# Order of splits, squares and first sums in the rounds of a norm ahead of a wide feed-forward stage

## The chip, the cores and the metric

The kernel runs on one core of a Trainium2 chip, in float32 throughout. A core has a matrix engine (TensorE, PE in the profile, with its weight loads as PEld), a vector engine (VectorE, DVE), a scalar engine (ScalarE, ACT), a general engine (GpSimd, POOL) and a queue that issues transfers (SyncE, SP). Each works through its own list of instructions in order and waits for the others through semaphores. The metric is the time of one execution on the device in microseconds (us), as the median of several runs.

## The reference

Two transformer blocks in a row, over 1024 tokens of width 1024. Each has a mixer (attention of two kinds in the first; a pooling mixer and a neighbourhood attention in the second), an output projection added to the residual x, a norm, and a feed-forward part. The part at issue is the last one, which both blocks have:

```python
# first block, D_FF = 2816
x = x + jnp.einsum('bse,ed->bsd', mixed, w_out[l])
h = rms_norm(x, ffn_norm_g[l])
g = jnp.einsum('bsd,df->bsf', h, w_gate[l])
u = jnp.einsum('bsd,df->bsf', h, w_up[l])
x = x + jnp.einsum('bsf,fd->bsd', jax.nn.silu(g) * u, w_down[l])
...
# second block, D_FF_2 = 4096
x = x + jnp.concatenate([a, b], axis=-1) @ w_out[l]
h = rmsnorm(x, norm_mlp_g[l])
x = x + jnp.square(jax.nn.relu(h @ w_up[l])) @ w_down[l]
```

`rms_norm` multiplies each row by one over the root of its mean square (with 1e-6 added), and each column by a gain.

## The kernel before

The residual x lies in eight tiles of 128 tokens by 1024 columns. Matrix products run on operands in a faster float format. To keep float32 precision, each operand is split into a high part h, a copy of the source in that format, and a low part l, the source less h; a product is then three, h by h, h by l and l by h. `split` (L113) does this: the copy on ACT (L114), the subtraction on DVE or, if asked, on POOL (L115).

The wide stage, the product of the normed x with the gate and up weights (or the up weights alone), is `ffn` (L873), called once in each block. It doesn't multiply the matrices directly. It cuts both into quadrants and forms seven products instead of eight, of sums and differences of quadrants. The tokens' side gives seven operands, named `b11` and `b21` (plain quadrants of the first four tiles: left and right half of the columns), `b22` (a plain quadrant of the last four), and `t1` to `t4` (differences). The weights' side gives `a11`, `a12`, `a22` and `s1` to `s4`. A unit is 256 columns of weights; there are 22 in the first block and 16 in the second.

Ahead of the units stand eight rounds, one for each tile t (L934 to L952). A round does the following.

- `down` (L179): PE multiplies the last quarter of the mixer's output with the last quarter of the output weights, 12 matmuls into two PSUM banks, and DVE adds these to x[t] (L195).
- x[t] is stored to `xd`, by SP (L936), since the scaling below overwrites it.
- ACT squares x[t] and sums each row (L938); POOL makes the mean (L939) and takes the power -1/2 (L941).
- DVE scales the tile of the round before, x[t-1], by its factor and the gain (`scaled`, L931).
- In rounds 3 to 6, the tile x[t-3], long scaled, is made into its share of `b11` and `b21` by two calls of `turn_split` (L778): PE transposes four blocks into a PSUM bank (L782), ACT copies the high part, DVE subtracts for the low part.
- In some rounds a weight piece is loaded (`load_raw`, L786).
- Half of a unit's `a11`, `a12` is split (`w_split`, L791): the copy on ACT, the subtraction on POOL.

Behind the rounds come `sums(0)`, `scaled(7)`, the first products `p1(0)` and `p1(1)`, and so on (L974 to L993). `sums(j)` (L961) forms, in place where it can, the differences of tile j and tile j+4: two subtractions on DVE, then two on POOL that read what the first two wrote (L732). `turn(j)` (L970) makes the five operands `b22`, `t1`, `t2`, `t3`, `t4` of these by five calls of `turn_split`; the last two read what POOL wrote. `p1(i)` (L915) is the product of `a11` and `b11` for unit i, whose result ACT copies aside (L920); `p2(i)` (L922) adds that of `a12` and `b21`. `w_sums` (L797) forms the differences of a unit's weights on POOL, and `w_rest` (L807) splits them; the main loop over the units follows at L1021.

What sets the order: the whole of this part runs under a manual schedule (L912 to L1131 for ACT, DVE, POOL and SP, L1513 for PE), so each engine's list has the instructions in the order in which the program names them. The PSUM has eight banks, taken through `one` (L107).

Of the kernel before, what the change touches and what calls it, by code (L numbers as in the profile page):

```python
# [11 lines left out]
AF = mybir.ActivationFunctionType  # L12
ALU = mybir.AluOpType
# [4 lines left out]
NT = 8  # L18
NK = 8
S = 1024  # L20
EPS = 1e-6
# [64 lines left out]
class Kern:  # L86
# [786 lines left out]
    def ffn(self, x, xd, mxd, wo, close_w, gi, n, gated, wts, wd, md, finish):  # L873


        nc, tc = self.nc, self.tc
        E = mybir.EngineType
        L = self.AHEAD
# [7 lines left out]
        slot = lambda: op.tile([P, 4, 512], F32R, tag="o", name="o")  # L886
        two = lambda tag: (aB.tile([P, 4, 512], F32R, tag=tag + "h", name=tag + "h"),
                           aB.tile([P, 4, 512], F32R, tag=tag + "l", name=tag + "l"))
# [5 lines left out]
        ops = [(pair(a_[0]), pair(a_[1]), [(pair(w_[0])[:, k, :], pair(w_[1])[:, k, :]) for k in range(2)])]  # L894
        jg = f32(flat(slot()))
        self.acts = {"b11": (slot(), slot()), "b21": (slot(), slot())}
        junk, g = jg[:, :S], jg[:, S:]
# [12 lines left out]
        us = [{"use": f} for f in users]  # L910
        first = lambda i: self.load_raw(wts[i][:, :1024])
# [16 lines left out]
        raws = [first(0), first(1)]  # L928
        r = [None] * NT

        def scaled(t):  # L931
            nc.vector.scalar_tensor_tensor(x[t], x[t], r[t], g, ALU.mult, ALU.mult)

        for t in range(NT):  # L934
            self.down(x, ops, t)
            nc.sync.dma_start(xd[t], x[t])  # L936
            ss, v = self.stat(), self.stat()
            nc.scalar.activation(junk, x[t], AF.Square, accum_out=ss)  # L938
            nc.gpsimd.tensor_scalar(v, ss, 1.0 / S, EPS, ALU.mult, ALU.add)  # L939
            r[t] = self.stat()  # L940
            nc.gpsimd.tensor_tensor(r[t], v, self.mhalf, ALU.pow)  # L941
            if t:
                scaled(t - 1)
            if 3 <= t < 7:
                self.turn_split(x[t - 3][:, :512], "b11", t - 3)
                self.turn_split(x[t - 3][:, 512:], "b21", t - 3)
            if t in (2, 4, 6):
                raws.append(first(t // 2 + 1) if t < 6 else self.load_raw(wts[0]))
            k = t % 2
            self.w_split(us[t // 2], ("a11", "a12")[k], raws[0][:, k * 512:(k + 1) * 512], True)  # L950
            if k:
                raws.pop(0)  # L952
        raws.append(first(L))

        for nm in ("t2", "t3"):
            self.acts[nm] = (slot(), slot())
        for nm in ("b22", "t1", "t4"):
            self.acts[nm] = two(nm)
        ts = [None] * 4

        def sums(j):  # L961
            lo, hi = x[j], x[j + 4]
            t2 = misc.tile([P, 512], F32, tag="y", name="t2s", bufs=6)
            self.sub(lo[:, :512], hi[:, :512], lo[:, :512], False)
            self.sub(t2, hi[:, 512:], lo[:, :512], False)
            self.sub(hi[:, :512], hi[:, 512:], hi[:, :512])
            self.sub(lo[:, 512:], t2, lo[:, 512:])
            ts[j] = (("b22", hi[:, 512:]), ("t1", lo[:, :512]), ("t2", t2), ("t3", hi[:, :512]), ("t4", lo[:, 512:]))
# [2 lines left out]
            for nm, src in ts[j]:  # L971
                self.turn_split(src, nm, j)

        sums(0)  # L974
        scaled(7)
        p1(0)
        p1(1)
# [812 lines left out]
```

## Time and profile before

| | |
|---|---|
| median of 3 runs | 2293.58 us (2292.99 to 2294.38) |
| the profiled execution | 2293.09 us |
| its span in the profile | 2291.3 us |
| mean granted clock of TensorE | 0.992 of full |
| mean DMA rate | 150 GB/s |
| rounds of the norm, first block | about 585 to 616 us from the span's start |
| rounds of the norm, second block | about 1612 to 1643 us from the span's start |

The span is the time from the first to the last instruction in the profile, and the execution's time is a little longer. A row of a timeline has the start in us, the duration in us, the engine, the line, the operation, what it writes and reads, and how many instructions were merged into the row (x2); in brackets stands how long the engine was idle before it, and what ended that. A row of busy time by stretch has the stretch, its length, each engine's busy time with the number of instructions, the granted clock of PE as a share of full, the share of DMA and its rate in GB/s. Successive instructions of an engine overlap a little in the records (about 0.1 us), since each is shown up to the end of its last write; so the step from one start to the next is somewhat shorter than the duration.

### The profile page before, as it was taken

What the parts mean: (1) busy time and instruction counts of PE and PEld (TensorE: products, weight loads), DVE (VectorE), ACT (ScalarE), POOL (GpSimd) and SP (SyncE); (2) the same over time, 40 slices, a digit from 0 to 9 for tenths busy, and PEclk for the clock granted to TensorE, in tenths of its full rate; (3) what the DMA queues carried; (4) which work ended last, traced back from release to release, by engine and by line L of the source; (5) the groups of instructions that cost most, each with busy time, mean ns of one, the idle gap of its engine ahead of it and who ended that gap; (6) DMA issues with size and microseconds to landing.
All of it is one profiled execution on the core that took longest, in us unless ns stands there. A gap on an engine that the chain in (4) does not pass through costs nothing.

```text
span 2291.3 us, 30717 instructions
## 1 busy us (share of the span) xinstructions
PE 2209.7 (96%) x11148; PEld 1869.7 (82%) x11148; DVE 1494.5 (65%) x2510; ACT 996.4 (43%) x1826; POOL 810.6 (35%) x742
## 2 busy tenths in 40 slices
PE   8999999989999999999999899999999998999998
PEld 8888898867788888878887888888778887878886
DVE  6356666677754545457889725687744445688888
ACT  5245555644442323223333536663454444434333
POOL 1055656564432322242235302120432223233335
PEclk9999999999999999999999999999999999999999
DMA  6386574651424433346321379883335543633202
GB/s 243 131 223 202 157 214 143 193 172 51 166 72 142 135 115 108 116 143 244 133 69 55 86 208 264 230 256 130 120 118 166 166 139 138 275 147 129 74 37 83
DMA packets 129193, 343.43 MB, mean 150 GB/s; under 512 B 12681, under 2 KB 49929, under 8 KB 114193
## 3 DMA queue, kind: packets, MB, share of 16 engines
q1 hardware_dynamic: 128896, 341.20, 45.7%
q8 instruction: 88, 1.44, 0.3%
q14 instruction: 65, 0.52, 0.1%
q10 hardware_dynamic: 144, 0.26, 0.0%
HBM read 254.35 MB, written 87.06 MB: 149 GB/s over the span
## 4 chain that ended last, share of the span: by engine, by line
PE 70%; DVE 15%; issue 5%; POOL 4%; ACT 4%; DMA 2%; SPq 0%; ACTq 0%; DVEq 0%; POOLq 0%
PE one L743 27%; PE one L1233 16%; PE one L163 11%; PE one L175 5%; DVE o L115 4%; PE one L189 4%; DVE x L195 1%; PE one L288 1%; PE one L582 1%; DVE x L1238 1%; DVE e L243 1%; PE one L230 1%; PE one L231 1%; DVE wl L115 1%; PE one L1414 1%
## 5 line engine op out<-in xcount | busy, mean ns | idle before, releaser
L1233 PE MATMUL one<-o 128*128 128x512 f32 x2268 | 519.3, 390 | 12.3 <-DVE o L115 12.2
L1233 PEld LDWEIGHTS one<-o 128*128 128x128 f32 x2268 | 424.3, 188 | 106.2 <-DVE o L115 18.4
L743 PE MATMUL one<-o,wh 128*128 128x512 f32 x1216 | 308.0, 396 | 17.1 <-DVE u L1042 8.7
L115 DVE TENSOR_TENSOR wl<-raw,wh 128x512 fp32r<-128x512 f32 (+2 forms) x254 | 206.0, 825 | 137.3 <-ACT wh L114 137.2
L743 PEld LDWEIGHTS one<-o,wh 128*128 128x128 f32 x1216 | 230.3, 191 | 69.2 <-ACT f L861 7.0
L114 ACT ACTIVATE wh<-raw 128x512 fp32r<-128x512 f32 (+2 forms) x278 | 185.7, 698 | 78.6 <-POOL raw L732 46.2
L732 POOL TENSOR_TENSOR s<-raw 128x512 f32<-128x512 f32 x38 | 54.9, 1446 | 443.2 <-DMA raw<-in_wgu_dram 208.1
L743 PE MATMUL one<-o,wl 128*128 128x512 f32 x608 | 164.4, 393 | 0.0
L247 ACT ACTIVATE e<-e,st 128x768 f32<-128x768 f32 (+7 forms) x128 | 99.4, 776 | 134.8 <-DVE st L243 131.7
L1238 DVE TENSOR_TENSOR x<-x,one 128x512 f32<-128x512 f32 x184 | 121.8, 677 | 50.6 <-PE one L1233 50.4
L743 PEld LDWEIGHTS one<-o,wl 128*128 128x128 f32 x608 | 115.6, 190 | 24.4
L163 PE MATMUL one<-actH,wh 128*128 128x512 f32 x448 | 122.8, 396 | 0.2 <-DVE ptl L115 0.2
L163 PE MATMUL one<-actL,wh 128*128 128x512 f32 x448 | 122.8, 396 | 0.0
L163 PE MATMUL one<-actH,wl 128*128 128x512 f32 x448 | 122.4, 395 | 0.0
L1394 POOL TENSOR_SCALAR ne<-ne,st 128x384 f32<-128x384 f32 x64 | 39.3, 614 | 220.7 <-DVE st L249 209.8
L1062 DVE TENSOR_TENSOR u<-one,p 128x512 f32<-128x512 f32 x38 | 26.3, 691 | 138.6 <-PE one L743 138.6
L114 ACT ACTIVATE o<-tb 128x1024 fp32r<-128x1024 f32 (+1 forms) x42 | 42.7, 1030 | 164.9 <-DVE tb L732 164.9
L735 POOL TENSOR_TENSOR sa<-mq 128x1024 f32<-128x1024 f32 (+1 forms) x14 | 35.4, 2545 | 196.4 <-DVE o L115 52.9
L565 POOL TENSOR_SCALAR b<-negc,cT 128x640 f32<-128x640 f32 (+3 forms) x64 | 49.8, 779 | 153.3 <-DVE st L243 94.8
L732 POOL TENSOR_TENSOR raw<-raw 128x512 f32<-128x512 f32 x76 | 99.3, 1306 | 6.0
L845 ACT ACTIVATE f<-f 128x512 f32<-128x512 f32 x33 | 20.9, 632 | 184.3 <-DVE f L838 167.1
L861 ACT ACTIVATE f<-f 128x512 f32<-128x512 f32 x48 | 30.3, 632 | 156.1 <-DVE f L838 126.8
(256 smaller groups left out, 5006.5 us busy)
## 6 DMA issues: line engine op xcount, KB each, us to landing
raw<-in_wgu_dram SPq DMA_DIRECT2D x22, 1024.0 KB, 5.3
raw<-in_wup_dram SPq DMA_DIRECT2D x16, 1024.0 KB, 5.4
mr<-f SPq DMA_DIRECT2D x64, 256.0 KB, 4.5
raw<-in_wdn_dram SPq DMA_DIRECT2D x12, 1024.0 KB, 4.9
wq<-in_wdn_dram SPq DMA_DIRECT2D x12, 1024.0 KB, 8.8
nbias<-in_nab_dram SPq DMA_DIRECT2D x32, 384.0 KB, 4.3
mq<-mr SPq DMA_DIRECT2D x12, 1024.0 KB, 9.8
raw<-in_wgu_dram SPq DMA_DIRECT2D x22, 512.0 KB, 3.8
```

The costliest lines, as they stand in the source:

```text
L114: self.nc.scalar.activation(h, src, AF.Copy)
L115: (self.nc.gpsimd if pool else self.nc.vector).tensor_tensor(l, src, f32(h), ALU.subtract)
L163: self.nc.tensor.matmul(ps, lhsT=w_[:, k, cols:cols + P], rhs=ac[:, 4 * j + k, half * 512:half * 512 + 512], start=(n == 0), stop=(n == 23))
L175: self.nc.tensor.matmul(ps, lhsT=ac[:, 4 * j + k, t * P:(t + 1) * P], rhs=w_[:, k, :], start=(n == 0), stop=(n == 23))
L189: nc.tensor.matmul(dst[h], lhsT=a_[:, kk, t * P:(t + 1) * P], rhs=w_[:, h * 512:(h + 1) * 512], start=(n < 2), stop=(n >= last))
L247: nc.scalar.activation(e, e, AF.Exp, bias=mx, scale=-1.0, accum_out=sm)
L565: nc.gpsimd.tensor_scalar(b[:, :nk], nc_row[:, :nk], cT[:, qt, h:h + 1], 1.0, ALU.add, ALU.mult)
L732: (self.nc.gpsimd if pool else self.nc.vector).tensor_tensor(out, a, b, ALU.subtract)
L743: self.nc.tensor.matmul(ps, lhsT=l, rhs=r, start=(first and n == 0), stop=(n == total - 1), skip_group_check=True)
L1233: nc.tensor.matmul(ps, lhsT=l[:, sl], rhs=r[:, sb], start=(start and n == 0), stop=(n == total - 1), skip_group_check=True)
L1238: nc.vector.tensor_tensor(dst, dst, ps, op)
L1394: nc.gpsimd.tensor_scalar(e[:, hf, :], e[:, hf, :], r, 1.0, ALU.mult, ALU.mult)
```

## The change

In rounds 3 to 6 the two calls of `turn_split` move from behind the scaling to ahead of the square. `sums(0)` moves from behind the loop into round 7, ahead of the square, the mean, the power, and the scaling of x[6]; for this, the functions `sums` and `turn` are defined ahead of the loop. Nothing else changes: the same instructions are issued, on the same engines.

```diff
-        for t in range(NT):
-            self.down(x, ops, t)
-            nc.sync.dma_start(xd[t], x[t])
-            ss, v = self.stat(), self.stat()
-            nc.scalar.activation(junk, x[t], AF.Square, accum_out=ss)
-            nc.gpsimd.tensor_scalar(v, ss, 1.0 / S, EPS, ALU.mult, ALU.add)
-            r[t] = self.stat()
-            nc.gpsimd.tensor_tensor(r[t], v, self.mhalf, ALU.pow)
-            if t:
-                scaled(t - 1)
-            if 3 <= t < 7:
-                self.turn_split(x[t - 3][:, :512], "b11", t - 3)
-                self.turn_split(x[t - 3][:, 512:], "b21", t - 3)
-            if t in (2, 4, 6):
-                raws.append(first(t // 2 + 1) if t < 6 else self.load_raw(wts[0]))
-            k = t % 2
-            self.w_split(us[t // 2], ("a11", "a12")[k], raws[0][:, k * 512:(k + 1) * 512], True)
-            if k:
-                raws.pop(0)
-        raws.append(first(L))
-
-        for nm in ("t2", "t3"):
-            self.acts[nm] = (slot(), slot())
-        for nm in ("b22", "t1", "t4"):
-            self.acts[nm] = two(nm)
         ts = [None] * 4
 
         def sums(j):
...
-        sums(0)
+        for t in range(NT):
+            self.down(x, ops, t)
+            nc.sync.dma_start(xd[t], x[t])
+            if 3 <= t < 7:
+                self.turn_split(x[t - 3][:, :512], "b11", t - 3)
+                self.turn_split(x[t - 3][:, 512:], "b21", t - 3)
+            if t == 7:
+                sums(0)
+            ss, v = self.stat(), self.stat()
+            nc.scalar.activation(junk, x[t], AF.Square, accum_out=ss)
+            nc.gpsimd.tensor_scalar(v, ss, 1.0 / S, EPS, ALU.mult, ALU.add)
+            r[t] = self.stat()
+            nc.gpsimd.tensor_tensor(r[t], v, self.mhalf, ALU.pow)
+            if t:
+                scaled(t - 1)
+            if t in (2, 4, 6):
+                raws.append(first(t // 2 + 1) if t < 6 else self.load_raw(wts[0]))
+            k = t % 2
+            self.w_split(us[t // 2], ("a11", "a12")[k], raws[0][:, k * 512:(k + 1) * 512], True)
+            if k:
+                raws.pop(0)
+        raws.append(first(L))
+
+        for nm in ("t2", "t3"):
+            self.acts[nm] = (slot(), slot())
+        for nm in ("b22", "t1", "t4"):
+            self.acts[nm] = two(nm)
         scaled(7)
         p1(0)
         p1(1)
```

## The prediction

> **What bounds the kernel now.** I read the page first, then the busy time of TensorE (PE) in stretches around the two places that the change touches, then the timeline of each engine there.
>
> ```profile
> PE 2209.7 (96%) x11148; PEld 1869.7 (82%) x11148; DVE 1494.5 (65%) x2510; ACT 996.4 (43%) x1826; POOL 810.6 (35%) x742
> ```
>
> PE is busy for 96% of the span, so an edit elsewhere pays only where it closes a hole of PE. The rounds run twice. For each I asked the busy time, the granted clock (PEclk) and DMA by stretch, the first time near 600 us and the second near 1640 us:
>
> ```profile
> 596.00:610.50 14.50, 14.50 (x81) 1.00 0.59 206
> 610.50:612.40 1.90, 0.18 (x2) 1.00 0.55 220
> ...
> 617.95:623.70 5.75, 2.90 (x21) 0.92 0.29 91
> 623.70:630.45 6.75, 6.75 (x27) 0.81 0.00 0
> ...
> 1636.50:1638.60 2.10, 0.00 (x0) 1.00 0.45 185
> 1638.60:1645.85 7.25, 7.22 (x25) 0.76 0.67 239
> 1645.85:1649.60 3.75, 2.51 (x21) 1.00 0.47 140
> 1649.60:1655.20 5.60, 5.60 (x28) 1.00 0.00 0
> ```
>
> PE has no hole during the rounds; the holes come right behind them. PE's timeline says who ends them, the first time and the second:
>
> ```profile
> 610.04 0.61 PE L189 MATMUL one<-b22h,t1l 128*128 128x512 f32 x2
> 612.38 2.11 PE L743 MATMUL one<-o,wh 128*128 128x512 f32 x8 [1.72 <-ACT o L114]
> ...
> 617.95 1.03 PE L782 MATMUL one<-ident,x 128*128 128x128 f32 x8
> ...
> 621.27 0.66 PE L782 MATMUL one<-ident,x 128*128 128x128 f32 x4 [1.84 <-POOL x L732]
> ...
> 623.70 3.27 PE L743 MATMUL one<-o,wh 128*128 128x512 f32 x8
> ...
> 630.44 1.03 PE L782 MATMUL one<-ident,x 128*128 128x128 f32 x8
> ...
> 632.54 2.09 PE L743 MATMUL one<-o,wh 128*128 128x512 f32 x8
> ```
>
> ```profile
> 1635.88 0.61 PE L189 MATMUL one<-b22h,t1l 128*128 128x512 f32 x2
> 1638.63 2.64 PE L743 MATMUL one<-o,wh 128*128 128x512 f32 x8 [2.13 <-ACT o L114]
> ...
> 1649.62 2.09 PE L743 MATMUL one<-o,wh 128*128 128x512 f32 x8
> ...
> 1655.20 1.03 PE L782 MATMUL one<-ident,x 128*128 128x128 f32 x8
> ```
>
> L189 is `down`, L743 the first products p1 and p2, L782 the transposes of `turn`. p1(0) waits for ScalarE (ACT) to copy the last "b" operand; turn(0) then waits for GpSimd (POOL) to form the last two sums; and the first eight matmuls of p2(0) take 3.27 us where the same eight take 2.09 us at 632.54, at a clock of 0.81 in that stretch. The second time the slow clock (0.76) falls on p1.
>
> Why is the copy late? One round on VectorE (DVE), with rows of the round's start from both places, then ACT and POOL:
>
> ```profile
> 596.51 1.28 DVE L195 TENSOR_TENSOR x<-one,x 128x512 f32<-128x512 f32 x2
> ...
> 609.29 1.28 DVE L195 TENSOR_TENSOR x<-one,x 128x512 f32<-128x512 f32 x2
> 610.49 1.27 DVE L932 SCALAR_TENSOR_TENSOR x<-x,st,o 128x1024 f32<-128x1024 f32 x1
> 612.35 1.29 DVE L115 TENSOR_TENSOR o<-one,o 128x512 fp32r<-128x512 f32 x2 [0.59 <-ACT o L114]
> 613.56 1.28 DVE L195 TENSOR_TENSOR x<-one,x 128x512 f32<-128x512 f32 x2
> ...
> 615.95 0.68 DVE L732 TENSOR_TENSOR x<-x,x 128x512 f32<-128x512 f32 x1
> ...
> 618.29 1.80 DVE L932 SCALAR_TENSOR_TENSOR x<-x,st,o 128x1024 f32<-128x1024 f32 x1 [0.93 <-DMA xd<-x]
> 620.01 1.75 DVE L732 TENSOR_TENSOR x<-x,x 128x512 f32<-128x512 f32 x1
> ...
> 1622.77 1.27 DVE L195 TENSOR_TENSOR x<-one,x 128x512 f32<-128x512 f32 x2
> ```
>
> ```profile
> 610.69 1.06 ACT L938 ACTIVATE o<-x 128x1024 f32<-128x1024 f32 x1 [1.62 <-DVE x L195]
> ...
> 611.74 1.06 ACT L114 ACTIVATE o<-one 128x512 fp32r<-128x512 f32 x2
> ```
>
> A DVE round is 613.56 - 609.29 = 4.27 us: adds 1.20, scaling 1.27, a wait of 0.59, two subtractions 1.21. The wait exists because the copies (611.74) stand behind the square (610.69) in ACT's queue, and the square waits for the adds. A round on PE is 14.50 us over four, 3.63 us. So DVE falls 0.64 us behind in each of four rounds, though PE doesn't feel it until p1(0).
>
> **The change part by part.** No instruction is added or taken away, and no DMA: it is order alone, on ACT, DVE and POOL. PE's order stays, and so does SP's.
>
> *(a) The split ahead of the square, rounds 3 to 6.* ACT copies as soon as PE has transposed. `down` 7 ends at 610.04 + 0.45 = 610.49, and its six pairs of matmuls take 6 x 0.45 = 2.7 us, so PE's transposes of round 6 end by 607.8, so both copies (1.06) are done by about 608.7, beside the adds. DVE's wait of 0.59 goes and its round becomes 1.20 + 1.21 + 1.24 = about 3.64 us, PE's own pace. Round 3's adds start at 596.51 and don't move, so the subtractions of round 6 end near 596.51 + 3 x 3.64 + 2.4 = 609.8, and p1(0) finds its operands at 610.49. The second time: 1622.77 + 10.92 + 2.4 = 1636.1 against 1636.33. The price is that the scalings move back by 1.21 us; those that PE transposes three rounds later have some 3 us to spare (scaling 3 would end near 596.51 + 3.64 + 3.65 = 603.8; its transposes start near 606.9). Cost nothing, hidden by those 3 us; without them, PE would wait for what is over.
>
> *(b) sums(0) in round 7, ahead of the square, the power and the scaling.* On POOL its two subtractions now stand ahead of the statistics and the weight split of round 7; on DVE its two stand ahead of scaling 6.
>
> ```profile
> 609.14 1.29 POOL L115 TENSOR_TENSOR wl<-raw,wh 128x512 fp32r<-128x512 f32 x1 [0.66 <-ACT wh L114]
> 611.92 0.19 POOL L939 TENSOR_SCALAR st<-st 128x1 f32<-128x1 f32 x1 [1.50 <-ACT o L938]
> 612.20 0.55 POOL L941 TENSOR_TENSOR st<-st,cols 128x1 f32<-128x1 f32 x1
> ...
> 618.97 2.24 POOL L732 TENSOR_TENSOR x<-x 128x512 f32<-128x512 f32 x1
> 621.18 1.70 POOL L732 TENSOR_TENSOR x<-t2s,x 128x512 f32<-128x512 f32 x1
> ```
>
> These rows show DVE and POOL taking turns: the scaling takes 1.80 us at 618.29 beside POOL and 1.27 at 610.49 without; POOL's subtraction from 618.97 ends as the DVE one of 620.01, stretched from 0.68 to 1.75, gets going. I take whole turns, 1.25 us net for a POOL subtraction. Let B be the start of the second add of round 7: 596.51 + 0.60 + 4 x 3.64 = 611.7 the first time, 1637.9 the second. POOL's weight split of round 6 now follows scaling 5 and ends about B + 1.4, so sums(0) on DVE runs to B + 2.8; POOL's first to B + 4.0; scaling 6 takes its turn to B + 5.2; POOL's second ends at B + 6.5: 618.2 and 1644.4. PE wants that one (t4) after p1 and four fifths of turn(0): 5.57 (612.38 to 617.95) + 1.74 behind 610.49 and 1636.33, at 617.8 and 1643.6. That leaves waits of about 0.5 and 0.9 us; I take 0.6 and 1.0 with a hop between engines. Bounds: nothing, if the turns fall the other way, and 2.6 and 2.9 us if each subtraction takes the 2.24 of the row.
>
> [...]
>
> *(c) What is late next.* Power 7 and weight split 7 follow on POOL (B + 8.5), scaling 7 on DVE waits for them (B + 9.8), then sums(1) (DVE B + 11.1, POOL B + 13.6). turn(1) wants the last of these at 610.49 + 5.57 + 2.10 + 5.58 + 1.74 + 0.6 = 626.1, and B + 13.6 is 625.3; the second time 1652.3 and 1651.5. It just fits, by 0.8 us. The load of the next wide operand waits for weight split 7, about 1 us later than now; it is wanted only some 30 us on. The subtractions of turn(0), behind sums(1) on DVE, end near B + 14.1, and free their banks as turn(1) asks for them.
>
> *The sum.* From the end of `down` to turn(1) PE now takes 630.44 - 610.49 = 19.95 us, and 1655.20 - 1636.33 = 18.87. The work in it at full clock is 5.57 + 2.10 (turn, 630.44 to 632.54) + 5.58 (p2, 1649.62 to 1655.20) = 13.25. So 6.7 and 5.6 us, 12.3 together, are holes and slow clock. Less the new waits, 6.1 + 4.6 = 10.7 us. Of it 1.2 us (3.27 less 2.09) and 1.6 us (the 7.25 of the stretch on p1 less 5.57) are slow clock: it follows 1.84 and another 1.0 us of hole the first time and 2.13 us the second, while a 1.24 us hole in 1645.85:1649.60 is followed by 1.00. With holes of at most 1 us I take the clock as full.
>
> [...]
>
> Does the gain reach the end? Behind turn(1) PE works without a long hole until the first full unit of the main loop:
>
> ```profile
> 663.63 2.11 PE L743 MATMUL one<-o,wh 128*128 128x512 f32 x8 [0.83 <-ACT p L920]
> ```
>
> That wait hangs on a weight load that starts when the split of the weight before it is done, itself behind turn(3) on ACT; so it moves along with PE. The profiled execution took 2293.09 us, its span 2291.3; the median of the runs is 2293.58. I apply the same 10.7 us to the median: 2282.9.
>
> **The rivals.**
>
> *The turns cost more.* Each POOL subtraction takes the 2.24 us of the row: waits of 2.6 and 2.9 us, and behind them the slow clock comes back for 1.2 and 1.6. The gain is 12.3 - 5.5 - 2.8 = 4.0 us: 2289.6, at the edge of what can be told from no change. For it: that row. Against: there DVE had three two-input operations in line, in round 7 it has one behind sums(0).
>
> *The slow clock stays.* The two slow stretches have another cause than the holes, and come again. The gain is 10.7 - 2.8 = 7.9: 2285.7. Against: both stretches start within 3 us of a hole. [...]
>
> *The gain is swallowed.* PE arrives earlier and waits as much longer at the first unit of the main loop, for a load bound by something that doesn't move, or the order on the engines doesn't change as written. 2293.6. For it: the wait at 663.63 shows that another chain is close there. Against: each link of it starts from PE's transposes.
>
> *Slower.* The place is (c): POOL's power 7 behind sums(0) delays scaling 7, sums(1) and turn(1). It decides once the last sum of sums(1) is more than 6.7 and 5.6 us later than PE wants it. If every POOL and DVE operation of that chain is stretched as in the worst rows (five POOL operations by 1.0, two sums of DVE and two scalings by about 1.0 and 0.5, the small ones by 0.8 together), it ends at about B + 22.4, 634.1 and 1660.3, where PE without other waits wants it at 625.5 and 1651.3: 8.6 + 9.0 - 12.3 = 5.3 us slower, and 8.1 with the slow clock behind the holes: 2301.7. Against: a turn can't stretch both sides at once.
>
> **How the numbers follow.** Forecast 2282.9: 0.64, its own range 2280.5 (no new wait, 12.3, and some 0.8 for the small wait at 663.63) to 2285. Turns cost more: 0.10. Slow clock stays: 0.08. Swallowed: 0.14. Slower: 0.04. The range reaches from 2280.5 to 2290.0 and leaves out the last two, 0.18. About 0.2%, 4.6 us, is what a measurement of this kernel can tell from no change. Faster: 0.64 + 0.08 + half of 0.10, 0.77; slower 0.04; the rest, 0.19, within.
>
> **What would show it.** (a) is right if DVE's rounds are 3.6 to 3.7 us and p1(0) starts without a wait for ACT near 610.5; wrong if DVE still waits for ACT's copies in each round. (b) is right if turn(0)'s waits for POOL are 1 us or less, wrong at 2 or more. (c) shows as no wait of turn(1) for POOL. The clock should read 1.00 from 596 to 625. The prediction is wrong if PE's wait at the first unit of the main loop grows by what was won, or if a hole opens inside the rounds, before the transposes.

## The result, and the profile after

| | before | changed |
|---|---|---|
| median of 5 runs, side by side | 2293.60 us (2292.99 to 2297.01) | 2282.25 us (2278.46 to 2285.75) |
| the profiled execution | 2293.09 us | 2282.18 us |
| its span | 2291.3 us | 2280.4 us |

The ratio is 0.9946, with a 95% interval of 0.9935 to 0.9957: 12.4 us faster (9.9 to 14.9). In a second comparison (e5 below) it was 0.9948 (0.9934 to 0.9961).

The page of the changed kernel, busy time by engine, and then PE by stretch: from the end of `down` to turn(1) in each block, and behind the first unit's wait (stretch, length, busy time, granted clock, DMA share, GB/s):

```profile
PE 2209.3 (97%) x11148; PEld 1872.4 (82%) x11148; DVE 1493.1 (65%) x2510; ACT 996.3 (44%) x1826; POOL 816.5 (36%) x742
```

```profile
608.90:622.10 13.20, 13.20 (x70) 1.00 0.48 167
656.30:661.70 5.40, 5.38 (x17) 0.68 0.01 3
1633.30:1646.65 13.35, 13.35 (x70) 1.00 0.52 172
```

From the end of `down` to turn(1) PE is busy without a hole, at full clock, in both blocks: 13.1 us (622.09 - 608.96) and 13.3 us (1646.63 - 1633.33), where it took 19.95 and 18.87. The first rounds start 1.5 us earlier in this profile (584.33, before 585.83), so steps are to be compared, and not times. PE's timeline of the changed kernel, at the landmarks shown before:

```profile
608.51 0.62 PE L189 MATMUL one<-b22h,t1l 128*128 128x512 f32 x2
608.96 1.98 PE L743 MATMUL one<-o,wh 128*128 128x512 f32 x8
...
615.72 1.04 PE L782 MATMUL one<-ident,x 128*128 128x128 f32 x8
616.51 2.10 PE L743 MATMUL one<-o,wh 128*128 128x512 f32 x8
...
622.09 1.03 PE L782 MATMUL one<-ident,x 128*128 128x128 f32 x8
```

```profile
1633.33 1.98 PE L743 MATMUL one<-o,wh 128*128 128x512 f32 x8
...
1640.08 1.22 PE L782 MATMUL one<-ident,x 128*128 128x128 f32 x8
1641.05 2.09 PE L743 MATMUL one<-o,wh 128*128 128x512 f32 x8
...
1646.63 1.03 PE L782 MATMUL one<-ident,x 128*128 128x128 f32 x8
```

No bracket is left: p1(0) follows `down` at its own pace, and so does p2(0) turn(0), but for some 0.2 us in the second block, where the transposes of 1640.08 take 1.22 instead of 1.04 (the last four need POOL's last sum, which ends at 1640.58). The reason on DVE, ACT and POOL, rounds 6 and 7:

```profile
605.76 1.27 DVE L195 TENSOR_TENSOR x<-one,x 128x512 f32<-128x512 f32 x2
606.96 1.27 DVE L115 TENSOR_TENSOR o<-one,o 128x512 fp32r<-128x512 f32 x2
608.15 1.27 DVE L932 SCALAR_TENSOR_TENSOR x<-x,st,o 128x1024 f32<-128x1024 f32 x1
609.35 1.27 DVE L195 TENSOR_TENSOR x<-one,x 128x512 f32<-128x512 f32 x2
610.55 1.37 DVE L732 TENSOR_TENSOR x<-x,x 128x512 f32<-128x512 f32 x1
611.95 0.69 DVE L732 TENSOR_TENSOR t2s<-x,x 128x512 f32<-128x512 f32 x1
612.56 2.32 DVE L932 SCALAR_TENSOR_TENSOR x<-x,st,o 128x1024 f32<-128x1024 f32 x1
```

```profile
605.96 1.09 ACT L114 ACTIVATE o<-one 128x512 fp32r<-128x512 f32 x2 [0.72 <-PE one L782]
607.15 1.06 ACT L958 ACTIVATE o<-x 128x1024 f32<-128x1024 f32 x1
```

```profile
610.07 1.30 POOL L115 TENSOR_TENSOR wl<-raw,wh 128x512 fp32r<-128x512 f32 x1
612.00 1.80 POOL L732 TENSOR_TENSOR x<-x 128x512 f32<-128x512 f32 x1 [0.63 <-DVE x L732]
613.76 2.26 POOL L732 TENSOR_TENSOR x<-t2s,x 128x512 f32<-128x512 f32 x1
```

DVE's round is 609.35 - 605.76 = 3.59 us, all work; before it was 4.27 with a wait of 0.59. The copies of 605.96 wait for PE alone and are over before the square (now L958). sums(0) and the scaling take turns with POOL, as the stretched rows show (1.37 for 0.68, 2.32 for 1.27, 2.26 for 1.28). POOL's last sum ends at 616.02, and PE takes it up at 616.15.

Not all of the gain in that stretch arrived in this execution. At the first unit of the first main loop, the changed kernel's PE:

```profile
656.32 2.59 PE L743 MATMUL one<-o,wh 128*128 128x512 f32 x8 [1.87 <-ACT p L920]
```

The wait was 0.83 before; now it is 1.87, with the slow clock (0.68) behind it: 2.7 us given back on the way to the second unit. e5 asks whether that belongs to the change.

All experiments and both kernels have the same 11148 matmuls on PE. The edits reorder a few of them only in e6 and e8, behind turn(1), so that the times between the same matmuls can be set side by side. The table has the step from one matmul of the first round (at 585.83 and 1612.33 before) to the first of turn(1), and from there to the second unit of the main loop, in us, for the first and the second block, worked out from the starts in the traces; then the ratio to runs of the kernel before that were taken beside it (their medians: 2293.60 for changed, 2293.62 for e1 to e4, 2295.08 for e5 and e6, 2294.55 for e8). The steps are those of one traced execution each.

| run | to turn(1) | to the second unit | median, ratio (95%) |
|---|---|---|---|
| before | 44.61 / 42.87 | 38.76 / 40.59 | 2293.6 |
| changed | 37.76 / 37.34 | 41.44 / 40.17 | 2282.25, 0.9946 (0.9935 to 0.9957) |
| e1 split only | 40.05 / 43.32 | 38.96 / 39.70 | 2286.52, 0.9959 (0.9941 to 0.9978) |
| e2 sums only | 39.83 / 41.31 | 39.05 / 41.04 | 2288.45, 0.9975 (0.9962 to 0.9989) |
| e3 copies ahead | 37.75 / 37.28 | 39.05 / 40.71 | 2281.55, 0.9935 (0.9913 to 0.9958) |
| e4 subtractions ahead | 48.22 / 48.45 | 38.90 / 40.56 | 2302.54, 1.0030 (1.0018 to 1.0042) |
| e5 changed again | 37.76 / 37.59 | 38.68 / 39.82 | 2281.60, 0.9948 (0.9934 to 0.9961) |
| e6 early rest | 37.79 / 37.56 | 39.09 / 37.80 | 2278.51, 0.9934 (0.9919 to 0.9950) |
| e7 before again | 45.80 / 43.15 | 39.34 / 40.25 | one run, 2297.62 |
| e8 early all | 37.76 / 37.52 | 36.70 / 36.62 | 2276.65, 0.9915 (0.9900 to 0.9930) |

The changed kernel takes 6.85 + 5.53 = 12.4 us less to turn(1), and the ratio says 12.4, with 9.9 to 14.9 around it. That the two agree to a tenth is chance: set against e7, the kernel before once more, the same steps give nearly 14. Elsewhere in the program, where nothing was changed, two executions differ by 2 to 4 us: between the two blocks' rounds by 943.1 us before, 945.8 changed, 947.3 in e7.

### The profile page after: what moved, and what is told of

The parts are those of the page before. It is cut to its first block, busy times and chain, and to the rows that moved or that the text cites. A ratio compares the mean times of both kernels' runs of the same rounds, so it can differ in the third digit from the quotient of the medians.

```text
span 2280.4 us, 30721 instructions
## 1 busy us (share of the span) xinstructions
PE 2209.3 (97%) x11148; PEld 1872.4 (82%) x11148; DVE 1493.1 (65%) x2510; ACT 996.3 (44%) x1826; POOL 816.5 (36%) x742
## 4 chain that ended last, share of the span: by engine, by line
PE 75%; DVE 13%; issue 4%; ACT 3%; POOL 3%; DMA 1%; SPq 0%; ACTq 0%; DVEq 0%; POOLq 0%
PE one L743 28%; PE one L1234 17%; PE one L163 12%; PE one L175 5%; PE one L189 5%; DVE o L115 4%; PE one L288 1%; PE one L582 1%; DVE x L195 1%; DVE e L243 1%; DVE x L1239 1%; PE one L231 1%; PE one L230 1%; PE one L1415 1%; ACT e L247 1%
## 5 line engine op out<-in xcount | busy, mean ns | idle before, releaser
L743 PE MATMUL one<-o,wh 128*128 128x512 f32 x1216 | 304.3, 392 | 13.5 <-DVE u L1043 8.3
L115 DVE TENSOR_TENSOR wl<-raw,wh 128x512 fp32r<-128x512 f32 (+2 forms) x254 | 206.3, 826 | 139.2 <-ACT wh L114 139.1
L845 ACT ACTIVATE f<-f 128x512 f32<-128x512 f32 x33 | 20.9, 632 | 185.3 <-DVE f L838 168.1
L195 DVE TENSOR_TENSOR x<-one,x 128x512 f32<-128x512 f32 x128 | 82.3, 680 | 24.3 <-PE one L189 24.1
```

Source lines behind the costliest of these rows:

```text
L115: (self.nc.gpsimd if pool else self.nc.vector).tensor_tensor(l, src, f32(h), ALU.subtract)
L195: nc.vector.tensor_tensor(xs, p_, xs, ALU.add)
L743: self.nc.tensor.matmul(ps, lhsT=l, rhs=r, start=(first and n == 0), stop=(n == total - 1), skip_group_check=True)
```

## The experiments

Each edit is shown against the changed kernel.

**e1, the splits alone.** sums(0) goes back behind the loop.

```diff
-            if t == 7:
-                sums(0)
...
+        sums(0)
         scaled(7)
```

> The splits stand ahead of the square as in the changed kernel; sums(0) stands behind the loop as before. Theory (the two edits need each other: with sums(0) late, the statistics and the weight split of round 7 and scaling 7 stand ahead of its two subtractions on POOL): p1(0) starts without a wait in both blocks, but turn(0) then waits for POOL 3 us or more in each, with slow clock behind it, and the gain over before is about 2 us (0 to 5). Rival (the edits add up, each closes its own hole): the holes ahead of p1(0), 1.9 and 2.3 us, and the slow clock on the second p1, 1.6 us, go, and turn(0) waits no longer than before: 6 us faster than before.

The stretch to turn(1) fell by 4.56 us in the first block and grew by 0.45 in the second, 4.1 together. p1(0) started without a wait in both. turn(0) waited for POOL twice in the first block, with full clock (1.00 from 616.90 to 622.50) behind it; the second time it was worse than before. PE in the first block, and in the second:

```profile
614.31 0.66 PE L782 MATMUL one<-ident,x 128*128 128x128 f32 x4 [0.32 <-POOL x L732]
616.51 0.66 PE L782 MATMUL one<-ident,x 128*128 128x128 f32 x4 [1.54 <-POOL x L732]
```

```profile
1641.01 0.66 PE L782 MATMUL one<-ident,x 128*128 128x128 f32 x4 [1.87 <-POOL x L732]
1642.68 1.12 PE L782 MATMUL one<-ident,x 128*128 128x128 f32 x4 [1.01 <-POOL x L732]
1643.45 3.76 PE L743 MATMUL one<-o,wh 128*128 128x512 f32 x8
```

So p1 is freed, but PE comes to turn(0) sooner than the sums do, and in the second block of this execution all of it is given back: 2.9 us in holes, and 2.5 us of slow clock on p2, which took 8.05 us for 5.58, at a clock of 0.67. The rival has turn(0) waiting no longer than before; in the second block it waited longer (2.9 us, before 1.24). The theory has 3 us of holes and the slow clock in the first block too, where it was 1.9 us at full clock. The time doesn't decide between them. It fell by 0.41% (0.22 to 0.59), which is 9.4 us (5.0 to 13.5), and the medians lie 7.1 apart: above the theory's 0 to 5 us, nearer the rival's 6, and more than the 4.1 of the traced execution, the slowest of the five. The waits are shown; what this edit alone is worth is not.

**e2, the early sums alone.** The two calls of `turn_split` go back behind the scaling.

```diff
-            if 3 <= t < 7:
-                self.turn_split(x[t - 3][:, :512], "b11", t - 3)
-                self.turn_split(x[t - 3][:, 512:], "b21", t - 3)
             if t == 7:
                 sums(0)
...
             if t:
                 scaled(t - 1)
+            if 3 <= t < 7:
+                self.turn_split(x[t - 3][:, :512], "b11", t - 3)
+                self.turn_split(x[t - 3][:, 512:], "b21", t - 3)
```

> sums(0) stands in round 7 as in the changed kernel; the splits of rounds 3 to 6 stand behind the scaling as before. Theory: p1(0) waits for ACT's copy as before, 1.7 and 2.1 us, with slow clock behind the second; turn(0) waits for POOL 0.6 us or less: 4.5 us faster than before (3 to 6). Rival (the edits add up, 12.4 less 6): 6.5 us faster. A third way, that early sums(0) alone is the change: 10 us or more.

4.78 and 1.56 us less to turn(1), 6.3 together, and 0.25% of the time (0.11 to 0.38), 5.7 us. PE in the first block:

```profile
611.18 2.14 PE L743 MATMUL one<-o,wh 128*128 128x512 f32 x8 [1.70 <-ACT o L114]
...
618.11 1.04 PE L782 MATMUL one<-ident,x 128*128 128x128 f32 x8
```

The copy's hole stays, turn(0) waits no more. The sum lies between theory and rival, which were too close to be told apart by it. What tells them apart is each block, by one execution of each kernel: e1 and e2 give 4.56 + 4.78 = 9.3 in the first, where both together give 6.85, and -0.45 + 1.56 = 1.1 in the second, where together they give 5.5. In the first block their gains overlap: each alone leaves the clock full behind turn(0) (1.00 in e1; in e2 the first eight matmuls of p2(0) take 2.10 us), and e1 shortens a wait for POOL that e2 takes away. In the second they need each other: to turn(1) either one alone takes longer than the two together, by 5.98 us in e1 (43.32 - 37.34; 2.9 of it holes, 2.5 slow clock) and by 3.97 in e2 (41.31 - 37.34).

**e3, ACT's order alone.** The copies stay ahead of the square, the subtractions go behind the scaling.

```diff
+            lows = []
             if 3 <= t < 7:
-                self.turn_split(x[t - 3][:, :512], "b11", t - 3)
-                self.turn_split(x[t - 3][:, 512:], "b21", t - 3)
+                lows = [self.turn_copy(x[t - 3][:, :512], "b11", t - 3),
+                        self.turn_copy(x[t - 3][:, 512:], "b21", t - 3)]
...
             if t:
                 scaled(t - 1)
+            for low in lows:
+                low()
```

(`turn_copy` transposes and copies, and returns the subtraction, to be issued later.)

> The changed kernel, but the low-part subtractions on DVE stand behind the scaling as before; only ACT's copies stay ahead of the square. Theory (ACT's order is what counted: the copy behind the square made DVE wait 0.59 us in each round): DVE's round is 3.6 us without a wait, p1(0) starts without a wait, and the time is that of the changed kernel within 1.5 us, 11 us faster than before. Rival (the order on DVE counted, since the subtraction has to be ahead of the scaling to be there for p1): p1(0) waits for DVE about 1 us, and with the slow clock behind it 3 to 4 us of the gain are gone in the two blocks together.

As the theory has it: 37.75 and 37.28 us, the changed kernel's own. DVE's timeline (the subtraction is L794 here, the scaling L942):

```profile
608.51 1.27 DVE L195 TENSOR_TENSOR x<-one,x 128x512 f32<-128x512 f32 x2
609.70 1.27 DVE L942 SCALAR_TENSOR_TENSOR x<-x,st,o 128x1024 f32<-128x1024 f32 x1
610.90 1.27 DVE L794 TENSOR_TENSOR o<-one,o 128x512 fp32r<-128x512 f32 x2
612.10 1.27 DVE L195 TENSOR_TENSOR x<-one,x 128x512 f32<-128x512 f32 x2
```

The round is 3.59 us again, without a wait, and p1(0) starts behind `down` without one, so the rival (DVE's order counted) is out.

**e4, DVE's order alone.** The subtractions stay ahead of the scaling, the copies go behind the square.

```diff
-            if 3 <= t < 7:
-                self.turn_split(x[t - 3][:, :512], "b11", t - 3)
-                self.turn_split(x[t - 3][:, 512:], "b21", t - 3)
...
             nc.gpsimd.tensor_tensor(r[t], v, self.mhalf, ALU.pow)
+            if 3 <= t < 7:
+                self.turn_split(x[t - 3][:, :512], "b11", t - 3)
+                self.turn_split(x[t - 3][:, 512:], "b21", t - 3)
             if t:
                 scaled(t - 1)
```

> The changed kernel, but ACT's copies stand behind the square as before; only the subtractions on DVE stay ahead of the scaling. Theory: DVE now waits for the square and both copies ahead of the subtractions, about 1.8 us in each round, its round is about 5.4 us, p1(0) starts 6 us or more later than in the changed kernel, and the time is 3 to 6 us above before. Rival (the order on DVE counted): as the changed kernel, 11 us faster than before.

0.30% slower than before (0.18 to 0.42), 6.9 us, and 3.6 + 5.6 = 9.2 us more to turn(1): the way that the theory has it, but more than its 3 to 6. DVE, then PE:

```profile
602.44 1.28 DVE L195 TENSOR_TENSOR x<-one,x 128x512 f32<-128x512 f32 x2
605.48 1.29 DVE L115 TENSOR_TENSOR o<-one,o 128x512 fp32r<-128x512 f32 x2 [1.76 <-ACT o L114]
606.68 2.19 DVE L932 SCALAR_TENSOR_TENSOR x<-x,st,o 128x1024 f32<-128x1024 f32 x1
608.79 1.28 DVE L195 TENSOR_TENSOR x<-one,x 128x512 f32<-128x512 f32 x2
```

```profile
609.02 1.06 PE L782 MATMUL one<-ident,x 128*128 128x128 f32 x8 [2.48 <-DVE x L932]
...
618.25 1.22 PE L743 MATMUL one<-o,wh 128*128 128x512 f32 x2 [5.36 <-ACT o L114]
```

The wait of 1.76 is the 1.8 that was expected. The round is 6.35 us and not 5.4, since the scaling takes 2.19 us for 1.27, about as long as where it stands beside POOL's work (2.32 at 612.56 in the changed kernel). Of the four orders this is the only one in which DVE's scaling, too, waits for ACT.

**e5, the changed kernel again**, with no edit.

> The changed kernel once more, unaltered. Theory (the 1.9 us wait of PE for ACT's copy at the first unit of the first main loop, and the slow clock behind it, came with one load that took 6.1 us instead of 5.1 in that one execution): the stretch from the end of the rounds to turn(1) again takes 13.1 and 13.3 us, and that wait is about 0.8 us, without slow clock behind it. Rival (the change itself moves the load and takes 2.7 us of its gain back there): the wait is again 1.5 us or more. Time about 11.5 us below before.

37.76 and 37.59 us to turn(1); the wait at the first unit is 0.8 us, at full clock, and the way to the second unit 38.68 us, where the first profile had 41.44. The wait, and the stretch behind it:

```profile
PE one L743 <- ACT p L920: 0.8, 1, 0.8
```

```profile
655.30:660.90 5.60, 5.60 (x25) 1.00 0.04 10
```

The load's row in the list of issues of the stretch ahead of that wait (size, and median us from issue to landing), in the changed kernel's first profile and in this one:

```profile
raw<-in_wgu_dram SPq DMA_DIRECT2D x1, 1024.0 KB, 6.1
```

```profile
raw<-in_wgu_dram SPq DMA_DIRECT2D x1, 1024.0 KB, 5.0
```

Issued 22.3 us after turn(1) each time, it landed a microsecond later in the first. So the 2.7 us given back were that execution's, not the change's.

**e6, a try at what is left.** The splits of the first unit's weights move ahead of turn(3), but for s4, and turn(3) makes t2 first (`turn` is given an order of its five operands for this).

```diff
         turn(2)
+        self.w_split(us[0], "a22", raws[0][:, 1536:])
         self.w_sums(us[0], raws.pop(0), misc)
         p2(2)
+        self.w_rest(us[0], "s3", "s1", "s2")
         p2(3)
-        self.w_rest(us[0], "s2", "s1")
-        turn(3)
-        self.w_rest(us[0], "s3", "a22", "s4")
+        turn(3, (2, 0, 1, 3, 4))
+        self.w_rest(us[0], "s4")
         raws.append(self.load_raw(wts[1]))
```

> The changed kernel, with the splits of the first unit's weights ahead of the last turn: a22 behind turn(2), s3, s1 and s2 between p2(2) and p2(3), s4 behind turn(3), and turn(3) makes t2 first. Theory (what is left behind the rounds are PE's waits at the first unit, for t2's copy behind two weight copies on ACT, 0.5 and 1.7 us, and for the load of the next weight, which starts when the last weight split is done, 0.8 to 1.9 and 1.1 us): both waits go in both blocks, 4 to 6 us faster than the changed kernel, about 16 us below before. Rival (another load, or POOL's sums of the next weights, ends just behind): the second wait stays as long, and the gain is 2 us or less.

The wait for t2 went in both blocks; the one at p2(4) did not (PE, then SP's issues):

```profile
657.45 2.11 PE L743 MATMUL one<-o,wh 128*128 128x512 f32 x8 [2.01 <-ACT p L920]
```

```profile
645.40 2.13 SPq L788 DMA_DIRECT2D raw<-in_wgu_dram  x2
```

The load was issued 645.40 - 623.93 = 21.5 us after turn(1), 0.85 us sooner only: it waits for the last split, s4, and that stood on DVE behind the five subtractions of turn(3). My 4 to 6 us had that split done at once. The load was also slow to land, 6.2 us, as in the first profile of the changed kernel, so a part of the 2.01 is this execution's; in the second block the wait is 0.9. The median is 3.1 us below that of e5, but the two intervals overlap.

**e7, the kernel before again**, with no edit.

> The kernel before, for a second profile. From the end of the rounds to turn(1) 19.9 and 18.9 us again, within 0.5 us, if the holes and the slow clock behind them are the kernel's own; the rest of the program shows how far two executions of one kernel lie apart (2 to 3 us expected between distant landmarks).

The holes are the same (1.73, 1.84 and 1.01 us in the first block), but p2 in the first block took 8.0 us at a clock of 0.68, where the first profile had 6.74. So the expected 0.5 us held in the second block (0.28), not in the first (1.19): the slow clock behind a hole isn't a fixed price: the clock read 0.50 for 3.41 us here in the first profile (from 622.83), and for about twice that in e7, 2 x (0.14 x 5.80 + 0.32 x 8.00) = 6.7 us by its rows. By stretch, turn(0) and then p2:

```profile
616.40:622.20 5.80, 2.94 (x21) 0.86 0.28 90
622.20:630.20 8.00, 8.00 (x27) 0.68 0.00 0
```

**e8, all splits early.**

```diff
+        self.w_sums(us[0], raws.pop(0), misc)
         sums(3)
         turn(2)
-        self.w_sums(us[0], raws.pop(0), misc)
+        self.w_rest(us[0], "a22", "s3", "s1")
         p2(2)
+        self.w_rest(us[0], "s2", "s4")
         p2(3)
-        self.w_rest(us[0], "s2", "s1")
-        turn(3)
-        self.w_rest(us[0], "s3", "a22", "s4")
         raws.append(self.load_raw(wts[1]))
+        turn(3, (2, 0, 1, 3, 4))
```

> The changed kernel, with POOL's sums of the first unit's weights ahead of sums(3), all five splits of them ahead of p2(2) and p2(3), the load of the next weight ahead of turn(3), and turn(3) making t2 first. In the run before, s4 stood behind turn(3) on DVE, so that load was issued only 0.85 us earlier and PE's wait at p2(4) stayed. Theory (that wait hangs on the time at which the load is issued): the load is issued some 6 us earlier, PE's waits for t2 (0.5 and 1.7 us) and at p2(4) (0.8 to 2.0 and 0.7 to 1.1 us) go in both blocks, 4 to 5 us faster than the changed kernel, 16 us below before. Rival (the load then ends on something else, or the longer row of splits pushes the last turn or the users of p2 back): a wait of 1 us or more stays at turn(3) or p2(4) in a block, and the gain over the changed kernel is 2 us or less.

2276.65 us, 0.9915 (0.9900 to 0.9930): it beats both kernels, and its interval lies clear of e5's (0.9934 to 0.9961). The load goes out at 641.67, 17.2 us after turn(1), so 5.1 us sooner than in the changed kernel, and PE has no wait left in either block between the rounds and the second unit; p2(4) follows at its own pace (SP's issues, then PE):

```profile
641.67 5.72 SPq L788 DMA_DIRECT2D raw<-in_wgu_dram  x2
```

```profile
655.73 1.98 PE L743 MATMUL one<-o,wh 128*128 128x512 f32 x8
```

To the second unit it takes 2.0 and 3.2 us less than e5, 5.2 together; the medians, taken in two comparisons, lie 4.95 apart, where 4 to 5 were expected.

## Why the prediction was right, step by step

The forecast was 2282.9 us, the result 2282.25, and the likeliest case came about. That the two lie within 0.7 us is in part luck: the new waits were put 1.4 us too high, the profile before had less slow clock than its repeat e7, and executions of one kernel differ by 2 to 4 us.

- *What bounds the kernel.* Right. The holes behind the rounds were what the change was worth: 12.4 us in the two stretches of the profiled executions, 12.4 by the ratio.
- *(a), the wait on ACT in each round.* Right, and shown. DVE's round went from 4.27 to 3.59 us (3.64 predicted), p1(0) starts without a wait, and PE has no hole in the rounds. e3 and e4 show that ACT's order did it: with the copies ahead of the square the place of the subtractions makes no difference, and with the copies behind it, subtractions ahead of the scaling make the kernel slower than before.
- *(b), sums(0) beside the scaling.* Right in kind: the rows show DVE and POOL taking turns again (POOL's two subtractions take 1.80 and 2.26 us, and 1.28 at 621.72). The size was off. The last sum came at B + 6.07 (B is 609.95 here), not B + 6.5, and B was 1.0 us behind the end of `down`, not 1.2. So the term "waits of 0.6 and 1.0 us" measured nothing in the first block and some 0.2 us in the second. It was bounded by nothing from below, so the range held it. e1 shows what the move itself takes away: without it, holes of 1.9 and 2.9 us.
- *(c), what is late next.* Right: no wait of turn(1) for POOL in either block, with 0.8 us to spare in both, as costed, though scaling 7 did wait for POOL:

```profile
616.96 2.31 DVE L932 SCALAR_TENSOR_TENSOR x<-x,st,o 128x1024 f32<-128x1024 f32 x1 [2.08 <-POOL st L961]
```

- *The slow clock.* The 2.8 us it was to bring back came back (2.9 by its own rows, since 7.25 less 5.57 is 1.68, not 1.6), and with no holes it read 1.00 there. The rival that it stays fell. Its size in the kernel before was one execution's: e7 has 2.4 us on p2 where the first profile had 1.2.
- *Does the gain reach the end?* Yes, but the sum left out that the first unit's wait can cost more in one execution than in another: 2.7 us more in the profiled one, for a load that landed 1.1 us late. The medians lie 11.35 us apart and the ratio says 12.4, give or take 2.5, so how much of that the other executions paid can't be told from them.

The rivals in which the gain is swallowed, the turns cost more, or the change is slower, are out: e5 has the gain again, and no chain behind the rounds takes it. Which of the two engines has its turn first differs between the blocks of e1. In the first, POOL's first sum, from 612.98, takes 1.27 us and its second 2.24; in the second block the scaling starts at 1638.54, 0.18 us ahead of the first sum, and takes 1.30, and the sum takes 2.24.

## What to carry to other kernels

In a queue that runs in order, look at which instruction stands ahead and what that one waits for: a square that waits for the adds held up a copy whose own operand had long been there, and with it a second engine, by 0.6 us in each of four rounds. A lag of an engine that isn't the bound costs nothing until the bound needs its last result (DVE's 0.64 us in each round cost PE nothing before p1(0), which waited 1.72 us), so read it where the stage ends, not where it arises. When a hole is closed, ask what the engine arrives at next: in the traced execution of e1, closing the first hole alone gave 4.6 us in one block and nothing in the other, since PE then waited for the sums; and once those came early, the next waits stood at the first unit (e8).

## What the runs showed of the hardware

- PE's clock read 0.50 behind some holes of about 2 us and 1.00 behind others. In the traces of the two kernels a slow stretch lasts 3.41 us or twice that, but for the one that the end of the trace cuts off, and within one trace the starts of the slow stretches lie whole multiples of 3.413 us apart (622.83 and 1640.00 in the kernel before: 1017.17 us, 298 of them). Counted in such steps, the hole of 1.87 us at the first unit of the changed kernel left PE busy for 1.54 us of one step, and the next step ran at 0.50; the hole of 1.72 us ahead of p1(0) in the kernel before left 1.69 us, and the next step ran at full clock:

```profile
654.34:657.75 3.41, 1.54 (x7) 1.00 0.02 5
657.75:661.16 3.41, 3.41 (x9) 0.50 0.00 0
```

```profile
609.18:612.59 3.41, 1.69 (x8) 1.00 0.38 142
612.59:616.01 3.42, 3.42 (x16) 1.00 0.98 359
```

  Around the two places (600 to 670 and 1630 to 1700 us), both traces fit this: steps at full clock with 1.54 us of work or less were followed by half clock, those with 1.69 or more were not. Elsewhere in the changed kernel's trace a step with 1.76 us (from 487.08) was followed by half clock and one with 1.58 (from 1913.86) was not, so it isn't a threshold. In e6 the hole at the first unit was longer, 2.01 us, and the clock behind it was full:

```profile
657.40:663.00 5.60, 5.55 (x24) 1.00 0.06 9
```

- The one-column statistics on POOL, 0.19 us at 611.92 in the kernel before, take 1.09 beside a scaling on DVE (608.15 to 609.42), here in round 6 of the changed kernel, and end with it, at 609.48, so here even the smallest operation took its turn.

```profile
608.39 1.09 POOL L959 TENSOR_SCALAR st<-st 128x1 f32<-128x1 f32 x1 [0.60 <-ACT o L958]
```

- Two executions of one program differ by 4.2 us in a stretch between the blocks (943.1 and 947.3 us, the kernel before and e7), and one load by 1.1 us in its landing (6.1 and 5.0 us, the changed kernel and e5).
- No run here times a product in plain float32, so that the format of the split operands (fp32r in the rows of L115) is the faster one is not shown.
